# A hybrid encoder block: r's projections computed whole, eight pairs of half products instead of twelve, and the sums of x made during the first mixer

## The chip, the core and the metric

The kernel runs on one core of a Trainium2 chip, in float32 (matrix products in float32r). The metric is the device time of one execution in microseconds, the median of several runs. A profiled execution gives a trace beside it: what each engine did and when, and what ended each wait. The engines are TensorE (PE in the profile; its weight loads PEld), VectorE (DVE), ScalarE (ACT), GpSimd (POOL) and SyncE (SP, which here only issues DMA transfers).

## What is computed

One encoder block on x of 1024 tokens and 1024 features. Cut to what matters:

```python
h = rms_norm(x, norm_mix_g)
proj = h @ w_in        # gla q, k, v, r; low-rank gate codes; swa q, k, v; gate_a, gate_b
o = gla(q, k, v, gates, forward) + gla(q, k, v, gates, backward)    # chunked linear attention, 4 heads
y_gla = (rms_norm(o, out_g) * silu(r)) @ w_o_gla
y_swa = windowed_attention(rope(rms_norm(sq)), rope(rms_norm(sk)), sv, sinks) @ w_o_swa
merged = sigmoid(gate_a) * y_gla + sigmoid(gate_b) * y_swa
x = x + merged @ w_out
x = x + (silu(h2 @ w_gate) * (h2 @ w_up)) @ w_ffn_out               # h2 = rms_norm(x, norm_ffn_g)
```

The columns of `w_in` that this document speaks of are r, gate_a (ga) and gate_b (gb), 1024 columns each: eight rows of 128 columns, `r0` to `r7` and so on.

## The kernel before

Every float32 product is made of three: an operand is split into a high part in float32r and the rest, h and l, and `h*h + h*l + l*h` is accumulated (`mm3`, or three `matmul` lines). A split costs one copy on ScalarE (L69, L756, L787) and one subtraction on VectorE (L71, L757, L788). The unit of work is a product of 128 x 128 by 128 x 512 (128 partitions, 512 values each); x lies in SBUF as `xh[k][s]`, `xl[k][s]` for eight blocks k of features and two halves s of the tokens.

TensorE's order is written out by hand; the other engines' orders come from a scheduler at build time, and each engine then works its list strictly in order, SP's list of DMA issues too. The program runs through these stages:

1. The norm of x, the projections q0 and k0, the low-rank gate codes.
2. **The GLA mixer**, in 45 time slots (`slot`, L263). A slot runs the small stages of the linear attention that are due (gates, scores, outputs, backward outputs, transposes) and puts n products of *filling* between them. The filling (`dense`, L543) is a list of generators: the projections that are still to be made, in the order they are needed. `GF` gives n for three ranges of slots. Where a stage needs a projection that isn't there yet, `need` pulls more filling.
3. **The attention mixer** (SWA) in 22 slots, the same way, with `SF`. Keys are prepared in the first eight (`k_prep`, `k_turn`), a block of four query heads in each of sixteen (`a_prep`, `a_turn`, `a_scores`, `a_probs`, `a_out`). `inv_norm` (L589) gets the squares' sums of each head from ScalarE with `accum_out`.
4. **Half products.** r, ga and gb are not all made as filling. The twelve `PAIRS` of rows (m and m + 4 of r, ga, gb) are computed with seven products of half size instead of eight. Two of the seven (`first_halves`, L221: one row's weights by the first half of the tokens, over all eight blocks k; 24 products a pair) are filling. After the attention comes `xsums`: it loads x again, scales it, and forms sums and differences of its quarters, named T1, T2, 22, T3, T4. The filling that is left runs (`fill(1 << 30)`, L877), then `second_halves` makes the other five products of a pair, 12 each (60 a pair): Z with T1, X with T2, X with T3, Z with 22, X with T4. X and Z are accumulators in PSUM (tags `mm` and `ch`). VectorE reads X after T2 (u2, L845) before T3 accumulates on it, and the results (L835) go to memory. From the fifth pair on, `prep_a` follows each pair: it loads r and the linear attention's output for one block, applies the sigmoid (ScalarE) and splits the result.
5. The output projections of both branches, the merge, `w_out`, and the feed-forward block, with the same half products. The change doesn't touch them.

A weight tile `wr` has four buffers, its parts `wh` and `wl` five. In `proj_t` the eight weight units of a projection are used twice, for the two halves of the tokens. `wkeep` (L149) writes both parts to memory after the first split, from GpSimd's queue; `wagain` (L158) loads them for the second half.

Of the kernel before, what the change touches and what calls it, by code (L numbers as in the profile page):

```python
# [14 lines left out]
P = 128  # L15
T = 1024
KT = 8
# [8 lines left out]
GF = (27, 20, 12)  # L26
SF = (40, 17, 17)
# [5 lines left out]
def body(tc, i, out):  # L33
    nc = tc.nc
    with ExitStack() as root:
# [77 lines left out]
        scr = {}  # L113
        glas = ExitStack()
# [103 lines left out]
        PAIRS = [(nme, m, r0, r0 + 4) for nme, base in (("r", 8), ("ga", 16), ("gb", 24))  # L218
# [31 lines left out]
        def fill(n):  # L250

            while n > 0 and dense:
                try:
                    next(dense[0])
                    n -= 1
                except StopIteration:
                    dense.pop(0)

# [274 lines left out]
        def g_turn(hd, c):  # L533
# [6 lines left out]
            for j in range(2):  # L540
# [4 lines left out]
                  proj_t("sq1", 4), first_halves()]  # L545
# [12 lines left out]
        with tc.manual_schedule(engines={mybir.EngineType.PE}):  # L558
            fill(24)
            for t in range(last + 1):  # L560
                n = GF[0] if t < 24 else GF[1] if t < NH * NC + 3 else GF[2]
                slot([(lambda v=at[t, j]: v[0](*v[1:])) if (t, j) in at else None for j in (0, 5, 4, 3, 2, 1)], n)
# [26 lines left out]
        def inv_norm(raw, n, sq, scale, epsv, eps_t):  # L589
            ss = sw.tile([P, n], F32, tag=f"ss{n}", name=nm("ss"))  # L590
            for h in range(n):
                nc.scalar.activation(sq[:, h], raw[:, h], AF.Square, accum_out=ss[:, h:h + 1])
# [147 lines left out]
        with tc.manual_schedule(engines={mybir.EngineType.PE}):  # L740
            for t, v in enumerate(todo):
                v.sort(key=lambda e: order.index(e[0]))
                slot([lambda e=e: e[0](*e[1:]) for e in v], SF[0] if t < 2 else SF[1] if t < 2 * KT + 2 else SF[2])
# [47 lines left out]
        def xsums(k):  # L791
            b = {}
            for q, kq, s in ((11, k, 0), (12, k, 1), (21, k + 4, 0), (22, k + 4, 1)):
                tag = f"n{q}{k if s == 0 else k % 2}"
                b[q] = tp.tile([P, HT], F32, tag=tag, name=nm(tag))
                nc.sync.dma_start(out=b[q], in_=i["xT"][kq, s])
                nc.vector.scalar_tensor_tensor(b[q], b[q], g1[:, kq:kq + 1], rstd[:, s * HT:(s + 1) * HT],
                                               op0=ALU.mult, op1=ALU.mult)
            nc.vector.tensor_tensor(b[12], b[12], b[11], op=ALU.subtract)
            XT["T1"].append(xsplit(xp, f"xh{k}1", f"xl{k}1", b[12]))  # L800
            XT["22"].append(xsplit(xp, f"xh{k + 4}1", f"xl{k + 4}1", b[22]))
            nc.vector.tensor_tensor(b[22], b[22], b[12], op=ALU.subtract)
            XT["T2"].append(xsplit(tp, f"t2h{k}", f"t2l{k}", b[22]))
            nc.vector.tensor_tensor(b[11], b[22], b[11], op=ALU.subtract)
            nc.vector.tensor_tensor(b[21], b[21], b[22], op=ALU.subtract)
            raws.append((b[11], b[21]))

        def xsums_late(k):
            XT["T3"].append(xsplit(xp, f"xh{k}0", f"xl{k}0", raws[k][0]))
            XT["T4"].append(xsplit(xp, f"xh{k + 4}0", f"xl{k + 4}0", raws[k][1]))  # L810

        nturn = [0]

        def ntile():
            q, k = divmod(nturn[0] % 8, 4)
            nturn[0] += 1
            tag = f"n{(11, 21)[q]}{k}"
            return tp.tile([P, HT], F32, tag=tag, name=nm("nt"))

        def put(key, t):  # L820
            d = scratch("_".join(map(str, key)))
            nc.sync.dma_start(out=d, in_=t)
            scr[key] = d

        def second_halves(f):
# [3 lines left out]
            r11, r21 = rawload(i["w_f"][a, 0], True), rawload(i["w_f"][b, 0], True)  # L829
            r12, r22 = rawload(i["w_f"][a, 1], False), rawload(i["w_f"][b, 1], False)  # L830
            Z, X = chtile((P, HT)), mmtile()

            def result(key, bank, add):
                t = stage()
                nc.vector.tensor_tensor(t, bank, add, op=ALU.add)  # L835
                put(key, t)

            s1 = comb(r21, r22, ALU.add)
            product(Z, wsplit(s1, 512), XT["T1"], 4, True, False)
            p5 = ntile()  # L840
            nc.vector.tensor_tensor(p5, Z, p1, op=ALU.add)
            s2 = comb(s1, r11, ALU.subtract)
# [3 lines left out]
            s3 = comb(r11, r21, ALU.subtract)  # L846
            product(X, wsplit(s3, 512), XT["T3"], 4, False, False)
            result((f"{nme}{m + 4}", 1), X, p5)
            s4 = comb(r12, s2, ALU.subtract)
            product(Z, wsplit(s4, 512), XT["22"], 4, False, True)  # L850
            result((f"{nme}{m}", 1), Z, u2)
            product(X, wsplit(r22, 512), XT["T4"], 4, False, True)
# [21 lines left out]
        with tc.manual_schedule(engines={mybir.EngineType.PE}):  # L874
            for k in range(4):
                xsums(k)
            fill(1 << 30)  # L877
            for k in range(4):
                xsums_late(k)
# [450 lines left out]
```

## Time and profile before

| | us |
|---|---|
| median of 3 runs | 1740.34 (1736.09 to 1740.75) |
| the profiled execution | 1737.7 |
| its span, first to last instruction | 1735.9 |
| TensorE busy | 1664.8 (96%) |
| VectorE busy | 1252.4 (72%) |
| ScalarE busy | 876.2 (50%) |
| GpSimd busy | 43.6 (3%) |

The page divides the span into 40 slices of 43.4 us and gives the busy share of each in tenths. A row of the stretches ("windows") has the length, then for each engine its busy time and number of instructions, the granted TensorE clock as a share of full speed, the DMA engines' share and their GB/s. A row of the waits has the instruction that waited, what released it, the total, the count and the longest. A row of the timeline has start, duration, engine, line, operation, output and inputs, and in brackets the idle time ahead of it and its releaser. A releaser is inferred, and where the engine named was done long before, it was another. Matmuls are pipelined: a product lasts 0.39 us in the timeline, though the next starts 0.23 us after it.

### The profile page before, as it was taken

Reading aid. Unit: us, or ns where it says so; the run is one execution under the profiler, and the core shown is the slowest. Engines: PE = TensorE matmul, PEld = TensorE weight load, DVE = VectorE, ACT = ScalarE, POOL = GpSimd, SP = SyncE. Lnnn points to the kernel's source line nnn. Section 1 sums busy time; section 2 is a strip of 40 time slices with the busy share of each in tenths; the row PEclk is TensorE's granted clock in tenths of the full one; section 3 lists DMA queues with packets and bytes.
Section 4 is the critical chain, followed back from the end, with each engine's and each line's share of the span. In section 5 each row is a group of like instructions: output and inputs, shape, how many; then the busy total and the mean of one; then the engine's idle time right before and its main releaser. Section 6 shows DMA issues by size and latency. Waiting matters only on the chain.

```text
span 1735.9 us, 23918 instructions
## 1 busy us (share of the span) xinstructions
PE 1664.8 (96%) x7740; PEld 1371.7 (79%) x7740; DVE 1252.4 (72%) x2586; ACT 876.2 (50%) x1957; POOL 43.6 (3%) x84
## 2 busy tenths in 40 slices
PE   9999999997999949988999999999999999999999
PEld 7788888886778737767788888888888888888887
DVE  8658687746898596665666466988777788789755
ACT  7546777765898642222455455733333333354442
POOL 1001010110000000000000000000000000000000
PEclk9999999998999979999999999999999999999999
DMA  7646566678243455444676455435223445396433
GB/s 274 214 140 196 181 194 207 213 241 282 91 141 110 145 183 170 150 141 148 222 224 194 151 161 161 128 128 163 92 103 130 149 135 175 127 334 207 133 116 116
DMA packets 174973, 293.85 MB, mean 169 GB/s; under 512 B 20510, under 2 KB 45854, under 8 KB 174848
## 3 DMA queue, kind: packets, MB, share of 16 engines
q1 hardware_dynamic: 168448, 271.35, 48.6%
q0 software_dynamic: 6400, 20.98, 3.3%
q8 instruction: 61, 1.00, 0.3%
q14 instruction: 64, 0.52, 0.1%
HBM read 201.02 MB, written 91.23 MB: 168 GB/s over the span
## 4 chain that ended last, share of the span: by engine, by line
PE 79%; DVE 9%; ACT 6%; DMA 4%; issue 2%; SPq 1%; ACTq 0%; DVEq 0%
PE mm L75 27%; PE mm L777 7%; PE mm L779 7%; PE mm L778 7%; PE mm L1148 7%; PE ch L75 6%; PE ch L1148 5%; PE ch L777 3%; PE ch L779 3%; PE ch L778 3%; PE mm L238 2%; DMA st<-r 2%; ACT p L692 1%; DMA wr<-in_w_f_dram 1%; DMA kvr<-skv 1%
## 5 line engine op out<-in xcount | busy, mean ns | idle before, releaser
L756 ACT ACTIVATE wh<-ws 128x512 fp32r<-128x512 f32 x136 | 86.0, 633 | 216.0 <-PE mm L778 106.2
L69 ACT ACTIVATE wh<-wr 128x512 fp32r<-128x512 f32 x190 | 119.0, 630 | 109.3 <-PE mm L75 85.3
L71 DVE TENSOR_TENSOR wl<-wr,wh 128x512 fp32r<-128x512 f32 x190 | 130.2, 687 | 43.1 <-ACT wh L69 40.7
L75 PE MATMUL mm<-wl,xh 128*128 128x512 f32 x320 | 129.4, 404 | 0.0
L75 PE MATMUL mm<-wh,xh 128*128 128x512 f32 x320 | 128.6, 402 | 0.1
L75 PE MATMUL mm<-wh,xl 128*128 128x512 f32 x320 | 128.4, 401 | 0.0
L757 DVE TENSOR_TENSOR wl<-ws,wh 128x512 fp32r<-128x512 f32 x136 | 93.2, 686 | 13.5 <-ACT wh L756 13.4
L756 ACT ACTIVATE wh<-wr 128x512 fp32r<-128x512 f32 x64 | 40.6, 634 | 113.8 <-issue 49.7
L756 ACT ACTIVATE wh<-a 128x512 fp32r<-128x512 f32 x66 | 41.9, 634 | 91.0 <-PE ch L1148 42.3
L757 DVE TENSOR_TENSOR wl<-a,wh 128x512 fp32r<-128x512 f32 x66 | 45.5, 691 | 40.1 <-ACT wh L756 39.0
L75 PEld LDWEIGHTS mm<-wh,xl 128*128 128x128 f32 x320 | 61.2, 191 | 10.4
L1148 PE MATMUL mm<-hh,wh 128*128 128x512 f32 x176 | 68.6, 390 | 0.5 <-DVE c L1086 0.5
L75 PEld LDWEIGHTS mm<-wh,xh 128*128 128x128 f32 x320 | 61.1, 191 | 10.0 <-ACT st L213 0.5
L1148 PE MATMUL mm<-hh,wl 128*128 128x512 f32 x176 | 68.5, 389 | 0.0
L1148 PE MATMUL mm<-hl,wh 128*128 128x512 f32 x176 | 68.5, 389 | 0.0
L75 PEld LDWEIGHTS mm<-wl,xh 128*128 128x128 f32 x320 | 61.3, 192 | 8.7
L238 PE MATMUL mm<-xh,wh 128*128 128x512 f32 x96 | 40.3, 420 | 19.9 <-ACT xh L787 19.9
L777 PE MATMUL mm<-xh,wh 128*128 128x512 f32 x96 | 40.9, 426 | 18.5 <-DVE nt L845 18.5
L770 DVE TENSOR_TENSOR ws<-wr,wr 128x512 f32<-128x512 f32 x68 | 46.9, 690 | 14.3 <-DMA wr<-in_w_f_dram 6.4
L1121 DVE TENSOR_TENSOR hl<-hr,hh 128x512 fp32r<-128x512 f32 x77 | 52.8, 687 | 5.6 <-ACT hh L1120 5.5
L75 PE MATMUL mm<-oah,wh 128*128 128x512 f32 x128 | 50.5, 395 | 3.1 <-ACT oah L787 3.1
L1120 ACT ACTIVATE hh<-hr 128x512 fp32r<-128x512 f32 x77 | 47.7, 619 | 8.1 <-DMA hr<-B 4.2
(552 smaller groups left out, 5120.3 us busy)
## 6 DMA issues: line engine op xcount, KB each, us to landing
wr<-in_w_fi_dram SPq DMA_DIRECT2D x102, 256.0 KB, 2.9
wr<-in_w_f_dram SPq DMA_DIRECT2D x88, 256.0 KB, 3.5
B<-c SPq DMA_DIRECT2D x44, 256.0 KB, 2.1
T<-st SPq DMA_DIRECT2D x44, 256.0 KB, 2.6
a<-in_w_fo_dram SPq DMA_DIRECT2D x44, 256.0 KB, 5.2
hr<-T SPq DMA_DIRECT2D x44, 256.0 KB, 2.6
wr<-in_w_t_dram SPq DMA_DIRECT2D x40, 256.0 KB, 3.2
wh<-wh POOLq DMA_DIRECT2D x40, 256.0 KB, 3.3
```

Source lines behind the costliest of these rows:

```text
L69: nc.scalar.activation(h, raw, AF.Copy)
L71: nc.vector.tensor_tensor(l, raw, h.bitcast(F32), op=ALU.subtract)
L75: nc.tensor.matmul(o, a, b, start=start, stop=stop)
L238: nc.tensor.matmul(Y[q], w[:, c], x, start=f0, stop=f1, skip_group_check=True)
L756: nc.scalar.activation(h, src, AF.Copy)
L757: nc.vector.tensor_tensor(l, src, h.bitcast(F32), op=ALU.subtract)
L777: nc.tensor.matmul(o, h[:, c], x[kk][0], start=start and kk == 0, stop=False, skip_group_check=True)
L778: nc.tensor.matmul(o, h[:, c], x[kk][1], start=False, stop=False, skip_group_check=True)
L779: nc.tensor.matmul(o, l[:, c], x[kk][0], start=False, stop=kk == nk - 1, skip_group_check=True)
L1120: nc.scalar.activation(h, r, AF.Copy)
L1121: nc.vector.tensor_tensor(l, r, h.bitcast(F32), op=ALU.subtract)
L1148: nc.tensor.matmul(ys[m], a[:, c], b, start=f0, stop=f1, skip_group_check=True)
```

## The change

- r is no longer among the pairs. Its eight rows are made whole (`proj_f`, 48 products a row) as filling, after `sq1` and before `first_halves`. `PAIRS` has the eight pairs of ga and gb.
- The sums of x are formed during the GLA mixer's first eight slots (`x_sums`) and written to memory; after the attention `xpart` loads them and splits them, and the first twelve are mixed with the filling that is left, `fill(4)` after each.
- A pair's products come in the order T1, T2, 22, T3, T4, and the T1 product of the next pair is placed ahead of T4. `prep_a` follows each of the eight pairs.
- The filling's numbers: 40 a slot in the first eight slots of the GLA mixer, then 27, 21 and 12; 60 in the first two slots of the attention, then 28 and 15.
- In `inv_norm` ScalarE makes one square of all heads, and VectorE sums them with a reduction.
- `wkeep` stores through SP instead of GpSimd, and GpSimd's DMA scratch is made smaller, which leaves room for the new tiles.

```diff
-GF = (27, 20, 12)
-SF = (40, 17, 17)
+GF = ((8, 40), (24, 27), (35, 21), (1 << 30, 12))
+SF = ((2, 60), (18, 28), (1 << 30, 15))
...
-                nc.gpsimd.dma_start(out=d, in_=v.bitcast(F32))
+                nc.sync.dma_start(out=d, in_=v.bitcast(F32))
...
-        PAIRS = [(nme, m, r0, r0 + 4) for nme, base in (("r", 8), ("ga", 16), ("gb", 24))
+        PAIRS = [(nme, m, r0, r0 + 4) for nme, base in (("ga", 16), ("gb", 24))
...
-                  proj_t("sq1", 4), first_halves()]
+                  proj_t("sq1", 4)] + [proj_f(f"r{m}", 8 + m) for m in range(8)] + [first_halves()]
+
+        xn = glas.enter_context(tc.tile_pool(name="xn", bufs=4))
...
+        def x_norm(k, s):
+            t = xn.tile([P, HT], F32, tag="xn", name=nm("xn"))
+            nc.sync.dma_start(out=t, in_=i["xT"][k, s])
+            nc.vector.scalar_tensor_tensor(t, t, g1[:, k:k + 1], rstd[:, s * HT:(s + 1) * HT],
+                                           op0=ALU.mult, op1=ALU.mult)
+            return t
+
+        def x_diff(key, k, d, a, b):
+            nc.vector.tensor_tensor(d, a, b, op=ALU.subtract)
+            put((key, k), d)
+
+        def x_sums(j):
+            k, late = divmod(j, 2)
+            if not late:
+                a, b = part[k] = x_norm(k, 0), x_norm(k, 1)
+                x_diff("xT1", k, b, b, a)
+                return
+            a, b = part.pop(k)
+            c = x_norm(k + 4, 1)
+            put(("x22", k), c)
+            x_diff("xT2", k, b, c, b)
+            x_diff("xT3", k, a, b, a)
+            c = x_norm(k + 4, 0)
+            x_diff("xT4", k, c, c, b)
...
+                if t < 8:
+                    x_sums(t)
...
-            for h in range(n):
-                nc.scalar.activation(sq[:, h], raw[:, h], AF.Square, accum_out=ss[:, h:h + 1])
+            nc.scalar.activation(sq, raw, AF.Square)
+            nc.vector.tensor_reduce(ss, sq, axis=mybir.AxisListType.X, op=ALU.add)
...
+        def xpart(q, k):
+            r = tp.tile([P, HT], F32, tag="xr", name=nm("xr"), bufs=8)
+            nc.sync.dma_start(out=r, in_=scr[f"x{q}", k])
+            pool, th, tl, d = homes[q]
+            XT[q].append(xsplit(pool, th.format(k + d), tl.format(k + d), r))
...
+        def second_first(f):
...
+            g.s1 = comb(g.r21, g.r22, ALU.add)
+            g.Z = chtile((P, HT))
+            product(g.Z, wsplit(g.s1, 512), XT["T1"], 4, True, False)
+
+        def second_rest(f):
...
+            nc.vector.tensor_tensor(p5, g.Z, p1, op=ALU.add)
+            X = mmtile()
+            s2 = comb(g.s1, g.r11, ALU.subtract)
+            product(X, wsplit(s2, 512), XT["T2"], 4, True, False)
+            u2 = ntile()
+            nc.vector.tensor_tensor(u2, X, p1, op=ALU.add)
+            s4 = comb(r12, s2, ALU.subtract)
+            product(g.Z, wsplit(s4, 512), XT["22"], 4, False, True)
+            result((f"{nme}{m}", 1), g.Z, u2)
+            s3 = comb(g.r11, g.r21, ALU.subtract)
+            product(X, wsplit(s3, 512), XT["T3"], 4, False, False)
+            result((f"{nme}{m + 4}", 1), X, p5)
+            if f + 1 < len(PAIRS):
+                second_first(f + 1)
+            product(X, wsplit(g.r22, 512), XT["T4"], 4, False, True)
+            result((f"{nme}{m + 4}", 0), X, p1)
...
-            for k in range(4):
-                xsums(k)
+            for q in ("T1", "T2", "22"):
+                for k in range(4):
+                    xpart(q, k)
+                    fill(4)
             fill(1 << 30)
+            second_first(0)
...
             for f in range(len(PAIRS)):
-                second_halves(f)
-                if f >= 4:
-                    prep_a(0, f - 4)
+                second_rest(f)
+                prep_a(0, f)
...
+    nc = _bacc.Bacc("TRN2", target_bir_lowering=False, num_devices=1, dynamic_dma_scratch_size=1024)
```

VectorE's order where the attention has ended and the last filling runs, before: `n` are x's quarters (L797 scales, L799 to L805 form the sums), `xl` and `t2l` their splits, and L241 is the read of a bank that the filling then goes on accumulating in.

```order
L797 SCALAR_TENSOR_TENSOR n_2058_8362<-n_2058_8362,g_70,rstd 128x512
L804 TENSOR_TENSOR n_2047_8331<-n_2050_8340,n_2047_8331 128x512
L788 TENSOR_TENSOR t2l_2056_8354<-n_2050_8340,t2h_2055_8353 128x512
L805 TENSOR_TENSOR n_2049_8337<-n_2049_8337,n_2050_8340 128x512
L797 SCALAR_TENSOR_TENSOR n_2059_8365<-n_2059_8365,g_70,rstd 128x512
L797 SCALAR_TENSOR_TENSOR n_2060_8368<-n_2060_8368,g_70,rstd 128x512
L799 TENSOR_TENSOR n_2058_8362<-n_2058_8362,n_2057_8359 128x512
L241 TENSOR_TENSOR st_8417<-mm_8247,rstd 128x512
```

The same place in the changed kernel, where L826 splits what was loaded (`xr`) and L247 is the read of a bank:

```order
L826 TENSOR_TENSOR xl_2079_8687<-xr_8684,xh_2078_8686 128x512
L247 TENSOR_TENSOR st_8711<-mm_8612,rstd 128x512
L826 TENSOR_TENSOR xl_2082_8697<-xr_8694,xh_2081_8696 128x512
L826 TENSOR_TENSOR xl_2085_8707<-xr_8704,xh_2084_8706 128x512
L71 TENSOR_TENSOR wl_8801<-wr_8797,wh_8799 128x512
L826 TENSOR_TENSOR xl_2092_8727<-xr_8724,xh_2091_8726 128x512
L247 TENSOR_TENSOR st_8751<-mm_8613,rstd 128x512
L826 TENSOR_TENSOR t2l_2095_8737<-xr_8734,t2h_2094_8736 128x512
L826 TENSOR_TENSOR t2l_2098_8747<-xr_8744,t2h_2097_8746 128x512
L247 TENSOR_TENSOR st_8793<-mm_8755,rstd 128x512
```

Before, 36 rows stood between two reads of banks; now two to four do, and the sums are gone from here.

VectorE's order within a pair with `prep_a`, before: `nt` from `ch` is p5, L870 the multiplication of r by its sigmoid (`sg`), L845 is u2, L871 and L788 the rest of `prep_a`, `ws` and `wl` the combined weights and their low parts for products ahead.

```order
L841 TENSOR_TENSOR nt_9235<-ch_9215,nt_9205 128x512
L757 TENSOR_TENSOR wl_9348<-ws_9345,wh_9347 128x512
L870 TENSOR_TENSOR st_9195<-st_9195,sg_9197 128x512
L845 TENSOR_TENSOR nt_9255<-mm_9216,nt_9205 128x512
L871 SCALAR_TENSOR_TENSOR st_9193<-st_9193,og,st_9195 128x512
```

And in the changed kernel, where L864 is p5, L869 u2, L896 the multiplication by the sigmoid, and L843 a result (from Z, `ch`, after the product with 22; from X, `mm`, after T4 of the pair before in the first such row, after T3 in the last):

```order
L864 TENSOR_TENSOR nt_9202<-ch_9149,nt_9198 128x512
L795 TENSOR_TENSOR wl_9279<-ws_9275,wh_9278 128x512
L808 TENSOR_TENSOR ws_9403<-wr_9399,wr_2272_9401 128x512
L843 TENSOR_TENSOR st_9182<-mm_9076,nt_9070 128x512
L795 TENSOR_TENSOR wl_9295<-wr_2210_9145,wh_9294 128x512
L869 TENSOR_TENSOR nt_9223<-mm_9204,nt_9198 128x512
L795 TENSOR_TENSOR wl_9336<-ws_9333,wh_9335 128x512
L808 TENSOR_TENSOR ws_9461<-ws_9403,wr_9397 128x512
L896 TENSOR_TENSOR st_9188<-st_9188,sg_9190 128x512
L843 TENSOR_TENSOR st_9243<-ch_9149,nt_9223 128x512
```

u2 now stands ahead of the multiplication by the sigmoid. After these rows come L897, `wl`, `ws`, the split `oal`, and the result of T3.

SP's order at the start of the GLA mixer in the changed kernel: L67 loads a weight unit (`wr`), L160 stores the two parts of an earlier one (GpSimd's queue did this before), L561 loads x for the sums.

```order
L561 DMA xn_712<-in_xT_dram 128x512
L160 DMA wh_0_530<-wh_526 128x512
L561 DMA xn_723<-in_xT_dram 128x512
L160 DMA wl_0_532<-wl_528 128x512
L160 DMA wh_1_540<-wh_536 128x512
L160 DMA wl_1_542<-wl_538 128x512
L160 DMA wh_2_550<-wh_546 128x512
L160 DMA wl_2_552<-wl_548 128x512
L160 DMA wh_3_572<-wh_568 128x512
L160 DMA wl_3_574<-wl_570 128x512
L67 DMA wr_632<-in_w_t_dram 128x512
```

Before, SP's list had the loads of eight units in a row here. Now the fifth stands behind the stores of the first four.

More of the change, by code (lines that the diff above doesn't have):

```diff
@@ L257, in fill, with share @@
                     dense.pop(0)
+        def share(plan, t):
+            return next(n for end, n in plan if t < end)
         def need(key):
@@ L789, in xsplit @@
             return h, l
[L791 to L806, printed above, removed]
@@ L827, in second_halves @@
+        def second_rest(f):
+            nme, m, a, b = PAIRS[f]
+            g = pend.pop(f)
             p1 = ntile()
             nc.sync.dma_start(out=p1, in_=scr[f"{nme}{m}", "p1"])
[L829 to L836, printed above, removed]
```

50 lines of the change are left out of this document (22 added, 28 removed).

## The prediction

> **What bounds the kernel now.** I read the page's slices first, then the busy time of each engine by stretches, then TensorE's waits, then the timelines at the two largest gaps.
>
> ```profile
> span 1735.9 us, 23918 instructions
> ...
> PE   9999999997999949988999999999999999999999
> ```
>
> TensorE is the bound almost everywhere; its lower digits stand between 390 and 860 us. The stretches below are cut at events of the program: the GLA mixer with its filling, the attention mixer (and its middle by itself), the filling that is left, the twelve pairs, and a long piece of what follows.
>
> ```profile
> core 0: us, PE busy (x) PEld busy (x) DVE busy (x) ACT busy (x) POOL busy (x), PEclk, DMA share, GB/s
> 60.00:403.50 343.50, 339.69 (x1862) 288.78 (x1860) 226.53 (x634) 221.41 (x617) 34.66 (x64) 1.00 0.62 201
> 403.50:598.40 194.90, 178.48 (x904) 144.68 (x903) 158.97 (x564) 165.30 (x530) 0.00 (x0) 0.96 0.42 133
> 480.00:540.00 60.00, 59.42 (x325) 49.54 (x324) 56.99 (x193) 58.88 (x192) 0.00 (x0) 1.00 0.46 141
> 598.40:638.20 39.80, 19.86 (x78) 15.94 (x77) 35.88 (x57) 18.76 (x30) 0.00 (x0) 0.74 0.70 231
> 638.20:835.30 197.10, 175.56 (x725) 140.65 (x724) 125.96 (x196) 47.34 (x76) 0.00 (x0) 0.96 0.47 148
> 860.00:1520.00 660.00, 660.00 (x2909) 545.87 (x2909) 486.73 (x780) 279.64 (x464) 0.00 (x0) 1.00 0.46 149
> ```
>
> The last row gives the price of a 128x512 product with nothing in its way: 660 us / 2909 = **0.227 us**. With it the other rows become losses.
>
> - Attention: 194.90 - 178.48 = 16.4 us idle, and a mean clock of 0.96 costs about 0.04 x 194.9 = 7.8 more: **24 us**.
> - The filling that is left: 39.8 us for 78 products (17.7): **22 us**.
> - The twelve pairs: 197.1 us for 12 x 60 products (163.4): **34 us**.
> - Up to 403.5 only 343.5 - 339.7 = **4 us** are lost.
>
> ```profile
> PE mm L238 <- ACT xh L787: 19.9, 1, 19.9
> PE mm L777 <- DVE nt L845: 18.5, 11, 2.5
> PE ch L634 <- issue: 4.3, 1, 4.3
> ```
>
> These are the waits of the three losing stretches. The first of them reads differently in the timelines of TensorE and VectorE:
>
> ```profile
> 612.92 0.39 PE L238 MATMUL mm<-xh,wl 128*128 128x512 f32 x1
> 633.25 0.77 PE L238 MATMUL mm<-xh,wh 128*128 128x512 f32 x1 [19.94 <-ACT xh L787]
> 633.82 0.63 PE L238 MATMUL mm<-xl,wh 128*128 128x512 f32 x1
> 634.24 0.63 PE L238 MATMUL mm<-xh,wl 128*128 128x512 f32 x1
> 607.23 0.75 DVE L797 SCALAR_TENSOR_TENSOR n<-n,g,rstd 128x512 f32<-128x512 f32 x1
> ...
> 632.42 0.69 DVE L241 TENSOR_TENSOR st<-mm,rstd 128x512 f32<-128x512 f32 x1
> 633.02 1.29 DVE L788 TENSOR_TENSOR xl<-n,xh 128x512 fp32r<-128x512 f32 x2
> ```
>
> The profile names ScalarE, but the product at 633.25 goes on accumulating in a bank that VectorE has to read first (L241, ended at 633.11). That read is 0.7 us of work, queued behind the sums of x that began at 607.23. VectorE starts a 128x512 operation every 0.60 us (632.42 to 633.02). And after the gap products start 0.42 us apart instead of 0.227; with about ten of them, a gap of over 2 us costs some 2 us more in the clock.
>
> **The change part by part.**
>
> *Products.* A pair costs 84 products (24 + 60), two whole rows 96. Four pairs become whole: 4 x 12 = 48 more, 48 x 0.227 = **+10.9 us**. Nothing hides them, since TensorE is the bound.
>
> *The sums of x, early.* VectorE's 16 scalings (0.75, L797) and 16 sums (0.69, L653 below), 23 us, move to the first eight slots of the GLA mixer. VectorE is busy 226.5 of 343.5 us there, and the filling of these slots grows from 27 to 40 products. Beside them go 16 loads and 20 stores, and the 80 stores of kept weights move from POOL's queue to SP's.
>
> ```profile
> wr<-in_w_t_dram SPq DMA_DIRECT2D x40, 256.0 KB, 3.2
> wh<-wh POOLq DMA_DIRECT2D x40, 256.0 KB, 3.3
> 603.68 0.80 SPq L796 DMA_DIRECT2D n<-in_xT_dram  x2
> ```
>
> SP then has in one line: a load, two stores that wait for that load's split, the next load. Below, this costs nothing, since weights are loaded up to four buffers ahead; it cannot gain, because nothing waits for POOL's stores and only 4 us are lost there. Above, the 36 new transfers hold back the loads behind them by their whole time to issue, 36 x 0.40 (0.80 for two) = 14 us. I take **+4**, nearer to the low end, because SP is late for no product in that stretch today.
>
> [...] No row here shows the kept stores on SP.
>
> *Attention.* The first two slots get 60 products instead of 40, the sixteen after them 28 instead of 17. In the program's order 498 filling products stand between the first transpose of the keys and the last product of the attention, against 320; the 178 x 0.227 = 40 us are only moved here. They lie on waits like the 4.3 us above.
>
> ```profile
> L712 ACT ACTIVATE ph<-ch 128x512 fp32r<-128x512 f32 x44 | 23.9, 595 | 1.5 <-PE ch L709 1.5
> L592 ACT ACTIVATE sq<-qr 128x128 f32<-128x128 f32 x64 | 19.3, 314 | 5.2 <-DMA qr<-sq 2.8 <-DVE qn L610 2.3
> L592 ACT ACTIVATION_READ_ACCUMULATOR sq<-qr 128x1 f32 x64 | 13.2, 206 | 0.0
> L653 DVE TENSOR_TENSOR qn<-qn,sq 128x512 f32<-128x512 f32 x16 | 11.0, 690 | 0.0
> ```
>
> From 480 to 540 ScalarE is busy 58.9 of 60 us, VectorE 57.0, TensorE 59.4: all three are near their end. The norm of q takes 4 x (0.314 + 0.206) = 2.1 us of ScalarE per block now, and one square of about 0.6 us (L712) afterwards. VectorE gets a reduction instead, which this trace doesn't have. Below, it costs nothing where VectorE waits anyway; above, twice a 128x512 operation, 1.4 us. I take 0.69, the row of L653, which passes as many values. A block then has ScalarE 1.5 us lighter, VectorE 0.7 heavier and TensorE 11 x 0.227 = 2.5 heavier. So TensorE becomes the longest in the later slots, and VectorE stays close to it in the eight that also prepare keys. Of the 24 us lost I leave 8 (ends 3 and 20): **-16**.
>
> [...]
>
> *The filling that is left.* 99 products follow the last product of the attention (which ended at 598.3), 22.5 us of cover. The loads of the sums still wait for the attention's memory, so I take today's delays: issue 5.3 us after that product (603.68), data 8.9 after it (607.23). In VectorE's new order no bank read stands behind more than two or three splits, so the 22 us go: **-22**.
>
> *The first pair.* From the first split of x to the weights of the third product (with s4) VectorE's order has 36 rows; at 0.60 they take 22 us and end 8.9 + 0.5 + 22 = 31 us after the attention. TensorE is there after 22.5 + 24 x 0.227 = 28 us. It waits 3 us, and the clock adds 2: 5 are left.
>
> *The other pairs.* Rows of TensorE, SP, ScalarE and VectorE around one gap:
>
> ```profile
> 740.37 0.39 PE L779 MATMUL mm<-t2h,wl 128*128 128x512 f32 x1
> 742.91 0.47 PE L777 MATMUL mm<-xh,wh 128*128 128x512 f32 x1 [2.15 <-DVE nt L845]
> 736.46 0.42 SPq L867 DMA_DIRECT2D st<-r  x1
> 740.81 0.63 ACT L869 ACTIVATE sg<-st 128x512 f32<-128x512 f32 x1 [2.27 <-DMA st<-r]
> 735.36 0.69 DVE L835 TENSOR_TENSOR st<-mm,nt 128x512 f32<-128x512 f32 x1 [0.70 <-PE mm L779]
> ...
> 741.47 0.69 DVE L870 TENSOR_TENSOR st<-st,sg 128x512 f32<-128x512 f32 x1 [2.10 <-ACT sg L869]
> 742.08 0.68 DVE L845 TENSOR_TENSOR nt<-mm,nt 128x512 f32<-128x512 f32 x1
> ```
>
> The third product (T3) needs u2 (L845), the read of the second one's bank. It stands behind the sigmoid of r, whose load is issued at 736.46. Afterwards the product with x22 lies between, 12 x 0.227 = 2.7 us, and u2 stands ahead of r's multiplication in VectorE's order. What is late next: T3's result must be read before T4 begins. The sigmoid ends 6.1 us after the last pair's T4 (735.3 to 741.4). From there seven rows of 0.60 put the end of T3's read at 10.3 us, and T4 begins at 48 x 0.227 = 10.9. It holds by half a microsecond, so I leave 0.5 us for each of seven pairs. With the first pair, 5 + 3.5 = 8.5 of 34 us are left (ends 4 and 27): **-25**. The wait for the last `prep_a` after the pairs stays.
>
> **Sum**, against the profiled execution's own 1737.7 us (the span of 1735.9 and 1.8 around it; the median of the runs, 1740.3, is 2.6 above): 1737.7 + 10.9 + 4 - 16 - 22 - 25 = 1689.6, so **1690 us**.
>
> **The rivals.**
>
> 1. *VectorE becomes the bound in the pairs.* For it: 17 rows of 0.60 are 10.2 of a pair's 13.6 us, in one order, with half a microsecond of slack at T4. Against: nothing but the load of r has to be late. If seven pairs keep today's 2.2 us and the clock's 2 instead of 0.5, that is 26 us more: **1716**.
> 2. *The gap only moves.* The sums come back from memory through the same queue. If the twelve loads that the first three products need land one after another, 12 x 3.2 = 38 us, the third product's operands come at 5.3 + 38 + 1.2 = 45 instead of 31 us, and the clock adds 2: **1706**. Against: eight buffers for them, and loads overlap at 603.68.
> 3. *Slower: SP starves the GLA mixer's filling.* A kept unit feeds 12 products, and TensorE now takes one in about 4.0 us (343.5 us for some 1040 filling products). If the next load goes out only when the stores before it have landed, a unit takes 3.2 + 3.3 = 6.5 us, and 40 units cost 40 x 2.5 = 100 us: **1790**. It outweighs the gains from 5.2 us a unit on. Against: four buffers, and a DMA share of 0.62.
> 4. *Everything closes*, all terms at their good ends (0, -21, -22, -30): **1676**.
>
> **How the numbers follow.** My forecast has 0.60, rival 1 0.20, rival 2 0.07, rival 3 0.05, rival 4 0.08. The range of 1672 to 1718 takes in all but rival 3 and a stack of several bad ends; the unknown prices (the reduction's 11 us, SP's 10) lie within it. A measurement of this kernel tells 0.3% (5.2 us) from no change. Faster by over that: 0.93, which is every case but rival 3 and a stack of bad ends on rival 1. Within it: 0.02. Slower: 0.05.
>
> **What would show it.** In the changed profile the wait of 19.9 us is gone, and no gap over 4 us stands between the attention's last product and the first pair's third; T3 no longer waits for u2; the keys' first transposes come at about 428 us, the attention's last product at about 646, the pairs' end at about 788 instead of 835. I am wrong if weight loads hold TensorE before 428 us (rival 3), if the pairs' products wait over 1 us each for VectorE (rival 1), or if the stages behind the pairs are not as long as before.

## The result, and the profile after

| | before | after |
|---|---|---|
| median of 4 runs, us | 1740.34 (1736.09 to 1740.75) | 1682.82 (1679.58 to 1685.03) |
| the profiled execution, us | 1737.7 | 1679.58 |
| its span, us | 1735.9 | 1677.3 |
| granted clock, mean | 0.983 | 0.996 |

The ratio of the times is 0.967 (95% interval 0.965 to 0.970). The forecast was 1690, with a range of 1672 to 1718.

The slices of the page, after, as they were shown of before:

```profile
span 1677.3 us, 23798 instructions
...
PE 1655.2 (99%) x7788; PEld 1372.9 (82%) x7788; DVE 1237.9 (74%) x2570; ACT 857.1 (51%) x1809; POOL 0.2 (0%) x4
...
PE   9999999999999998999999999999999999999999
```

One digit is still below 9, the sixteenth, where the pairs begin. The stretches, cut at the same events of the program (the columns are those of the table of before):

```profile
60.00:425.80 365.80, 362.55 (x1968) 308.26 (x1967) 253.06 (x694) 228.34 (x626) 0.00 (x0) 1.00 0.69 228
425.80:634.10 208.30, 206.60 (x1079) 173.75 (x1078) 167.76 (x564) 153.21 (x390) 0.00 (x0) 1.00 0.36 114
634.10:656.60 22.50, 22.50 (x100) 18.40 (x98) 14.49 (x23) 10.23 (x17) 0.00 (x0) 1.00 0.88 289
656.60:776.00 119.40, 114.37 (x486) 93.04 (x486) 93.38 (x147) 43.66 (x72) 0.00 (x0) 0.97 0.65 215
```

The attention now has 1.7 us of idle time and a full clock, and the filling that is left has none. Only the pairs still lose: 119.4 us for 480 products (109.0). TensorE's longest waits of the whole kernel:

```profile
PE ch L815 <- ACT wh L794: 4.6, 2, 2.6
PE mm L75 <- ACT oah L825: 3.2, 1, 3.2
PE ch L75 <- DVE lrS L313: 1.9, 1, 1.9
PE mm L75 <- DMA wl<-wl: 1.2, 1, 1.2
```

The waits of 19.9 us (last filling) and 18.5 us (T3 for u2) are gone. Where the time came from, stretch by stretch, at 0.227 us for each product that was added or taken away:

| stretch | length, us | products | its products' time | what else | predicted |
|---|---|---|---|---|---|
| to the first key transposes | 403.5 to 425.8 | +89 | +20.2 | **+2.1** | +4 |
| attention | 194.9 to 208.3 | +175 | +39.7 | **-26.3** | -16 |
| filling that is left | 39.8 to 22.5 | +22 | +5.0 | **-22.3** | -22 |
| pairs | 197.1 to 119.4 | -240 | -54.5 | **-23.2** | -25 |
| behind the pairs | 900.6 to 901.3 | 0 | 0 | **+0.7** | 0 |

The products are +10.4 in sum (the prediction had 10.9; these rows hold 46 of the 48 more that the page counts, 7788 against 7740), and all together makes -58.6, the difference of the spans. Before's first key transposes begin at 408.0, after a wait of 4.3 us; its stretch is cut where that wait begins, at 403.5, so the wait counts with the attention.

### The profile page after: what moved, and what is told of

Read it like the earlier page. It is cut to its first block, busy times and chain, and to the rows that moved or that the text cites. A ratio compares the mean times of both kernels' runs of the same rounds, so it can differ in the third digit from the quotient of the medians.

```text
span 1677.3 us, 23798 instructions
## 1 busy us (share of the span) xinstructions
PE 1655.2 (99%) x7788; PEld 1372.9 (82%) x7788; DVE 1237.9 (74%) x2570; ACT 857.1 (51%) x1809; POOL 0.2 (0%) x4
## 4 chain that ended last, share of the span: by engine, by line
PE 91%; DVE 3%; DMA 3%; ACT 2%; issue 1%; SPq 0%; ACTq 0%; DVEq 0%
PE mm L75 35%; PE ch L75 8%; PE mm L815 7%; PE mm L816 7%; PE mm L817 7%; PE mm L1177 7%; PE ch L1177 5%; PE ch L815 3%; PE ch L817 3%; PE ch L816 3%; PE mm L244 2%; PE ch L747 1%; DMA xr<-xT 1%; PE ch L546 0%; PE ch L697 0%
## 5 line engine op out<-in xcount | busy, mean ns | idle before, releaser
L71 DVE TENSOR_TENSOR wl<-wr,wh 128x512 fp32r<-128x512 f32 x198 | 135.7, 686 | 32.0 <-ACT wh L69 29.1
L794 ACT ACTIVATE wh<-ws 128x512 fp32r<-128x512 f32 x120 | 75.5, 631 | 148.7 <-PE mm L816 84.6
L75 PE MATMUL mm<-xh,wh 128*128 128x512 f32 x256 | 102.5, 401 | 0.3 <-ACT wh L69 0.3
L75 PE MATMUL mm<-xl,wh 128*128 128x512 f32 x256 | 102.0, 398 | 0.3 <-DVE xl L323 0.3
L795 DVE TENSOR_TENSOR wl<-ws,wh 128x512 fp32r<-128x512 f32 x120 | 82.1, 685 | 12.8 <-ACT wh L794 12.8
L75 PE MATMUL mm<-xh,wl 128*128 128x512 f32 x256 | 88.6, 399 | 0.0
L75 PEld LDWEIGHTS mm<-wl,xh 128*128 128x128 f32 x320 | 60.5, 189 | 12.6 <-DMA wl<-wl 1.6
L75 PEld LDWEIGHTS mm<-xl,wh 128*128 128x128 f32 x256 | 48.2, 188 | 7.6 <-DVE xl L323 0.6
L75 PEld LDWEIGHTS mm<-xh,wh 128*128 128x128 f32 x256 | 48.2, 188 | 7.4 <-ACT wh L69 0.5
```

The source lines that it names most:

```text
L71: nc.vector.tensor_tensor(l, raw, h.bitcast(F32), op=ALU.subtract)
L75: nc.tensor.matmul(o, a, b, start=start, stop=stop)
L794: nc.scalar.activation(h, src, AF.Copy)
L795: nc.vector.tensor_tensor(l, src, h.bitcast(F32), op=ALU.subtract)
```

## The experiments

Kernels measured together share a chip and its runs of before, whose median was 1739.6 us for e1 to e4, 1739.6 for e5 to e8, 1738.3 for e9 to e11 and 1740.6 for e12; the ratios are to these. The profiled execution is one of the runs, and not always near their median: e1's took 1740.7 us and was the slowest of its six. Four events of each profiled execution, in us: the first key transposes (A), the copy of the attention's last output (B), the last filling product (C), the last product of the pairs (D):

| kernel | median, us | ratio to before, 95% interval | A | B | C | D |
|---|---|---|---|---|---|---|
| before | 1740.3 | | 408.0 | 598.4 | 638.0 | 835.1 |
| after | 1682.8 | 0.9652 to 0.9695 | 425.8 | 634.3 | 656.4 | 775.7 |
| e1 SP stores only | 1733.8 | 0.9931 to 0.9978 | 404.1 | 593.2 | 632.8 | 836.3 |
| e2 new norm only | 1738.1 | 0.9978 to 1.0014 | 409.4 | 598.2 | 637.2 | 834.4 |
| e3 old norm | 1685.2 | 0.9654 to 0.9707 | 428.1 | 638.8 | 660.8 | 781.1 |
| e4 old attention filling | 1696.0 | 0.9728 to 0.9760 | 420.8 | 611.3 | 681.4 | 791.3 |
| e5 old order in a pair | 1702.5 | 0.9762 to 0.9809 | 425.3 | 633.8 | 655.8 | 798.4 |
| e6 late sums | 1708.3 | 0.9797 to 0.9839 | 419.9 | 629.0 | 652.3 | 802.3 |
| e7 twelve pairs | 1694.3 | 0.9712 to 0.9763 | 412.5 | 598.5 | 615.8 | 792.3 |
| e8 first pair eased | 1671.3 | 0.9586 to 0.9629 | 423.8 | 633.2 | 655.4 | 770.8 |
| e9 ten pairs | 1686.8 | 0.9676 to 0.9723 | 422.0 | 623.6 | 637.5 | 786.5 |
| e10 spread sums | 1675.3 | 0.9605 to 0.9656 | 431.1 | 641.1 | 663.1 | 777.6 |
| e11 e8 again | 1673.4 | 0.9593 to 0.9646 | 426.6 | 636.4 | 658.4 | 774.6 |
| e12 sums at the end | 1674.4 | 0.9607 to 0.9660 | 429.9 | 638.4 | 661.3 | 776.7 |

### What closed the attention: the norm or the filling (e2, e3, e4)

e2 makes this edit in the kernel before, e3 takes it back in the changed one:

```diff
-            for h in range(n):
-                nc.scalar.activation(sq[:, h], raw[:, h], AF.Square, accum_out=ss[:, h:h + 1])
+            nc.scalar.activation(sq, raw, AF.Square)
+            nc.vector.tensor_reduce(ss, sq, axis=mybir.AxisListType.X, op=ALU.add)
```

> The kernel before, with only the new norm of the heads: one square on ScalarE and one reduction on VectorE. Theory A, the attention's loss was closed by more filling between its stages: 1740 within 3 us, since VectorE gets 0.7 us a block and nothing covers it better. Theory B, ScalarE's four squares and four accumulator reads were what the attention waited for: most of its 24 us go, so 1718 to 1728, and the stretch of the attention falls from 195 to about 175 us.

> The changed kernel with the old norm of the heads put back (ScalarE squares with sums). Theory A (filling covers): ScalarE has 1.5 us more a block beside 4.5 us that TensorE is busy with filling, so 1683 to 1688. Theory B (the norm was the bound): the attention loses 12 to 24 us again, so 1695 to 1707.

e4 takes the attention's numbers back in the changed kernel:

```diff
-SF = ((2, 60), (18, 28), (1 << 30, 15))
+SF = ((2, 40), (1 << 30, 17))
```

> The changed kernel with the attention's old filling numbers (40 in two slots, then 17); the some 200 products not placed there run after the attention. Theory A (filling covers the stages' waits): the attention loses 12 to 26 us again, mostly as gaps of TensorE and a lower granted clock, so 1695 to 1709. Theory B (the norm did it): 1683 within 5 us.

The norm alone does nothing measurable (1738.1 against 1739.6, the interval holds 1), and its removal costs 2.4 us with intervals that overlap. The filling does it. e4 rose to 1696.0, as its theory A had it. Its attention and the filling left after it, from the stretches, and its waits in the attention:

```profile
420.80:611.50 190.70, 175.46 (x903) 141.77 (x902) 157.09 (x556) 149.58 (x384) 0.00 (x0) 0.98 0.33 102
611.50:681.60 70.10, 70.10 (x311) 58.00 (x310) 41.24 (x65) 27.46 (x45) 0.00 (x0) 1.00 0.80 263
681.60:791.50 109.90, 109.90 (x485) 90.76 (x484) 83.67 (x130) 34.73 (x56) 0.00 (x0) 1.00 0.56 187
...
PE ch L697 <- DVE mx L715: 4.8, 3, 2.8
PE ch L75 <- DVE mx L715: 3.3, 7, 1.8
PE ch L75 <- DVE kTl L675: 2.4, 1, 2.4
```

With 176 products less (40.0 us) the attention is only 17.6 us shorter (208.3 to 190.7): 22.4 us of its waits and of the lower clock after them (0.98) are back, 13.5 of them as idle time (15.2 us against 1.7). The third row is a gain that nobody had asked for: with 70 us of filling ahead of them the pairs lose nothing (109.9 us, no idle time). So the time rose by 13 us, not by 22.

Most of this happens while the keys are prepared. The stretch from the first key transposes to the last, in before, in after and in e4:

```profile
403.50:482.00 78.50, 65.90 (x312) 53.50 (x311) 66.75 (x270) 64.22 (x236) 0.00 (x0) 0.89 0.45 149
425.80:500.00 74.20, 74.20 (x389) 63.14 (x388) 73.29 (x271) 57.80 (x155) 0.00 (x0) 1.00 0.42 136
420.80:495.40 74.60, 63.25 (x311) 50.08 (x310) 70.48 (x273) 57.57 (x153) 0.00 (x0) 0.95 0.42 134
```

TensorE was idle for 12.6 us of it in before (4.3 of them the wait ahead of the first transposes) and for 11.4 in e4. In after it never was, although VectorE was busy 73.3 of the 74.2 us.

The reduction's price is in the groups of VectorE of the changed kernel (count, busy us, mean ns):

```profile
L630 DVE TENSOR_REDUCE ss<-sq 128x4 f32<-128x512 f32 x16 | 10.9, 681 | 0.0
```

The reduction takes 0.68 us, against the 0.69 that the prediction took and the 1.4 of its upper end. A `tensor_tensor` of the same 512 values takes 0.69 us (L71, 686 ns on the page).

### SP's queue and the sums in the GLA mixer (e1, e10, e12)

e1 is the kernel before with one edit:

```diff
-                nc.gpsimd.dma_start(out=d, in_=v.bitcast(F32))
+                nc.sync.dma_start(out=d, in_=v.bitcast(F32))
```

> The kernel before, with the stores of the kept weights issued from SP instead of GpSimd and nothing else changed. Theory A, the prediction's +4: SP's one line holds the loads back, the stretch up to the first key transposes grows by 2 to 5 us, so 1742 to 1746. Theory B, only the time to issue counts: SP has room, 1740 within 2 us. Rival C, each load waits for the landing of the stores ahead of it: 1790 or more.

All three miss: by the medians the kernel is faster, by 3.8 to 12.0 us. The products reach the first key transposes at the same time (404.1 against 403.5), but the 4.3 us that before then waited are gone. The operands of these transposes go back to the constants of the attention. SP's rows for the last of them and for the first keys and values, in before and then in e1:

```profile
388.76 2.01 SPq L67 DMA_DIRECT2D wr<-in_w_f_dram  x2
...
396.82 0.94 SPq L62 DMA_DIRECT2D sink<-in_sink_dram  x1
397.81 0.97 SPq L625 DMA_DIRECT2D kvr<-skv  x1
```

```profile
392.42 0.43 SPq L62 DMA_DIRECT2D sink<-in_sink_dram  x1
392.89 0.43 SPq L625 DMA_DIRECT2D kvr<-skv  x1
```

In e1 they go out 4 to 5 us earlier, with no weight loads just ahead of them and at half the time to issue, and the attention ends 5.2 us earlier (593.2 against 598.4). Where the median's gain lies stays open, since this execution was not faster as a whole: its pairs took 203.5 us from C to D against before's 197.1, which used the 5.2 us up.

e10 and e12 were to find the price of the sums in the first slots, on top of e8 (below):

```diff
-                if t < 8:
-                    x_sums(t)
+                if t < 24 and t % 3 == 1:    # e10
+                    x_sums(t // 3)
+                if 34 <= t < 42:             # e12
+                    x_sums(t - 34)
```

> The kernel of e8 with the sums of x formed in every third GLA slot from the second on (8 of the first 24) instead of in the first eight. Theory A (the sums cost the GLA mixer 4 to 6 us, as the first key transposes of e6 at 419.9 against 425.8 say, because VectorE's small stages of the first slots stand behind them): 1666 to 1669 and the first transposes at 420 to 422. Theory B (those 4 us are only the spread of single profiles): within 2 us of e8.

> The kernel of e8 with the sums of x formed in GLA slots 34 to 41 instead of 0 to 7. From 340 us on VectorE is busy less than half of the time in e8 (8.95 of 20 us from 340 to 360), against 45.7 of 60 from 60 to 120 us. Theory A (the sums cost 26 products' time in the first 120 us, since the small stages wait behind them and behind 1.9 times the DMA traffic): most of 5.9 us comes back, 1666 to 1669, with the first key transposes at 419 to 422. Theory B (their loads and stores, at a DMA share of 0.6 to 0.9 there, hold back the weights and the constants of the attention): 1673 or more.

Neither tells its theories apart, since the sums hardly moved; that e12's median lies in theory B's range says nothing for B. The subtractions of the sums in e8 and in e12 (count, least, median and longest ns, first and last start in us):

```profile
L567 DVE TENSOR_TENSOR xn<-xn,xn x16: 669/689/693, 45.6 to 109.4; 128x512 f32<-128x512 f32 x16
```

```profile
L567 DVE TENSOR_TENSOR xn<-xn,xn x16: 666/684/695, 46.9 to 129.0; 128x512 f32<-128x512 f32 x16
```

Only TensorE's order is that of the code. The scheduler orders VectorE's and SP's work, and it began the sums at the same place wherever the call stands; x and `rstd` are there from the start. The last of them ran some 20 us later, and the first key transposes came at 431.1 and 429.9, later than in any execution with the sums in the first slots (428.1 at most); why is not shown. The price of the sums comes from e6, which has none in the GLA mixer, and the same 2203 products up to the key transposes. The stretch from 60 to 120 us, in after and then in e6:

```profile
60.00:120.00 60.00, 58.89 (x297) 49.50 (x296) 44.14 (x97) 26.60 (x59) 0.00 (x0) 1.00 0.88 296
```

```profile
60.00:120.00 60.00, 60.00 (x309) 50.88 (x309) 33.74 (x84) 30.81 (x71) 0.00 (x0) 1.00 0.49 157
```

After has VectorE 10 us busier, 1.9 times the DMA traffic, and 12 products less, with 14 less in the 60 us ahead of it: 26 products are 5.9 us. e6 reaches the transposes at 419.9 instead of 425.8, and five executions with that part of the program alike lie between 423.8 and 428.1. So the sums cost about 6 us there (4 to 8, from one execution of e6). Whether VectorE or the DMA traffic makes the cost is not shown. A place for them that costs less wasn't found.

### The order of a pair (e5)

```diff
             u2 = ntile()
             nc.vector.tensor_tensor(u2, X, p1, op=ALU.add)
+            s3 = comb(g.r11, g.r21, ALU.subtract)
+            product(X, wsplit(s3, 512), XT["T3"], 4, False, False)
+            result((f"{nme}{m + 4}", 1), X, p5)
             s4 = comb(r12, s2, ALU.subtract)
             product(g.Z, wsplit(s4, 512), XT["22"], 4, False, True)
             result((f"{nme}{m}", 1), g.Z, u2)
-            s3 = comb(g.r11, g.r21, ALU.subtract)
-            product(X, wsplit(s3, 512), XT["T3"], 4, False, False)
-            result((f"{nme}{m + 4}", 1), X, p5)
-            if f + 1 < len(PAIRS):
-                second_first(f + 1)
             product(X, wsplit(g.r22, 512), XT["T4"], 4, False, True)
             result((f"{nme}{m + 4}", 0), X, p1)
+            if f + 1 < len(PAIRS):
+                second_first(f + 1)
```

> The changed kernel with the old order of a pair's products: T1, T2, T3, 22, T4, and T1 of the next pair after T4. Theory A (the order closed the pairs' gaps: u2 stands behind the sigmoid of r again, with no product in between): each of eight pairs waits 0.9 to 2.4 us ahead of T3 and pays up to 2 us in the clock, 1.1 to 4.2 a pair by the pair lengths of the kernel before, so the pairs take 126 to 150 us instead of 117 and the time is 1692 to 1716, nearer to the upper end. Theory B (r came out of the pairs, its results lie in memory long before, and that closed the gaps): only the bare read of the bank is left, 1683 to 1692.

Theory A, in the middle of its range. The edit takes both moves back, the place of the product with 22 and that of the next pair's T1; they were not tried one by one. The wait of before is back at its place, and the pairs take 140.1 us from the first product to the last instead of 117.0:

```profile
PE mm L815 <- DVE nt L869: 15.7, 8, 3.3
```

### The sums late (e6)

```diff
-                if t < 8:
-                    x_sums(t)
...
+            for t in range(8):
+                x_sums(t)
             for q in ("T1", "T2", "22"):
                 for k in range(4):
                     xpart(q, k)
                     fill(4)
```

> The changed kernel with the sums of x formed after the attention instead of in the first eight slots of the GLA mixer; they are still written to memory and loaded again. Theory A (VectorE's 32 operations of the sums at this place cost the 22 us): 19 us of VectorE and a way through memory of 5 to 6 us come back ahead of the splits, TensorE's cover is the same, and the filling or the first pair waits some 20 us: 1697 to 1710. Theory B (the filling between the loads, four products after each, keeps VectorE's reads of banks near, and that alone closes the gap): the filling doesn't wait, the first pair waits under 8 us more: 1683 to 1691.

Theory A. The filling hardly waits (1.1 us, theory B's part of it holds), but T1's operands come late, block by block:

```profile
PE ch L812 <- ACT xh L822: 30.3, 3, 11.2
```

The pairs take 149.7 us instead of 117.0, the GLA mixer gives 6 back, and 25.5 us are lost.

### r as half products again (e7, e9)

e7 puts r back among the pairs, with the old filling numbers of both mixers (`GF` 27, 20, 12 and `SF` 40, 17) and with `prep_a` from the fifth pair on; e9, on top of e8, does it for two of r's four pairs:

```diff
-        PAIRS = [(nme, m, r0, r0 + 4) for nme, base in (("ga", 16), ("gb", 24))
+        PAIRS = [(nme, m, r0, r0 + 4) for nme, base in (("r", 8), ("ga", 16), ("gb", 24))
```

> The changed kernel with r as four pairs again (twelve pairs, 48 products or 10.9 us less) and the old filling numbers of both mixers, since 288 filling products are gone. New order of a pair, early sums, new norm and SP stores stay. Theory A (the whole rows of r pay for themselves by covering the attention): the attention loses 12 to 24 us again, so 1684 to 1698, no faster than the changed kernel. Theory B (the other edits carry the gain, r as whole rows only costs): 1672 within 4 us.

> The kernel of e8 with two rows' pairs of r as half products again (ten pairs): 24 products less, 144 less filling, taken from the first eight GLA slots (33 for 40) and from the attention's slots 2 to 17 (24 for 28). Theory A (a filling product placed in the attention is worth 0.11 us on the average, 22.9 us for 202 in e4): 5.4 us gained, some 7 lost in the attention and some 2 elsewhere, 1671 to 1679. Theory B (the last products placed there cover nothing any more): 1664 to 1668.

e7 is 11.5 us slower with 10.9 us less to multiply. Its attention and its pairs:

```profile
412.50:598.60 186.10, 172.95 (x903) 140.72 (x902) 163.04 (x569) 152.75 (x394) 0.00 (x0) 0.99 0.44 145
...
616.00:792.50 176.50, 167.11 (x725) 137.69 (x724) 130.85 (x202) 59.03 (x94) 0.00 (x0) 0.97 0.59 196
```

Against after, the attention has 176 products (40.0 us) less and is 22.2 us shorter: 17.8 us are lost there. The first key transposes, at 412.5, come 9.0 us after before's 403.5 with one product more; with 27 filling products a slot instead of 40 the sums may cost more than the 6 us above. e9 misses both ranges on the side of A: 13.5 us over e11, the same base on the same chip. Its attention, its last filling and its pairs, and then e8's attention:

```profile
422.00:623.70 201.70, 195.70 (x1017) 162.20 (x1016) 165.32 (x551) 152.33 (x389) 0.00 (x0) 0.99 0.40 127
623.70:637.70 14.00, 14.00 (x64) 11.55 (x63) 11.34 (x18) 5.72 (x10) 0.00 (x0) 1.00 0.86 281
637.70:786.70 149.00, 141.15 (x605) 115.14 (x604) 113.11 (x176) 54.85 (x87) 0.00 (x0) 0.98 0.64 210
```

```profile
423.80:633.30 209.50, 207.40 (x1081) 173.79 (x1080) 168.87 (x568) 154.45 (x394) 0.00 (x0) 1.00 0.36 115
```

The attention lost 6.7 us by the same sum (64 products less are 14.5 us, and it is 7.8 shorter), as expected. But only 14.0 us of filling are left behind it, and the ten pairs take 149.0 us for 600 products (136.2): 12.8 lost against 6.4 in e8. And the first key transposes come 1.8 us earlier than e8's, 4.6 earlier than e11's, with 43 products (9.8 us) less, so 5 to 8 us are lost in the GLA mixer, where seven products a slot were taken from the slots that make the sums.

### The first pair (e8, e11)

What the changed kernel still waits for stands in these rows of TensorE and VectorE (start, duration, idle time in brackets):

```profile
658.72 0.50 PE L815 MATMUL ch<-xh,wh 128*128 128x512 f32 x1 [1.98 <-ACT wh L794]
669.40 0.50 PE L815 MATMUL ch<-xh,wh 128*128 128x512 f32 x1 [2.58 <-ACT wh L794]
656.66 0.68 DVE L826 TENSOR_TENSOR xl<-xr,xh 128x512 fp32r<-128x512 f32 x1
657.26 0.69 DVE L808 TENSOR_TENSOR ws<-wr,wr 128x512 f32<-128x512 f32 x1
664.54 2.29 DVE L826 TENSOR_TENSOR xl<-xr,xh 128x512 fp32r<-128x512 f32 x3 [0.16 <-ACT xh L825]
667.94 0.68 DVE L808 TENSOR_TENSOR ws<-wr,ws 128x512 f32<-128x512 f32 x1
```

Both sums of weights (`ws`) stand behind splits (`xl`) for products that come later: the first behind those for 22, the second (s4) behind those for T4. e8 moves them (`first_w` is the part of `second_first` ahead of its product), and makes the last two blocks of `prep_a` one pair earlier, the first three one pair later:

```diff
+                if q == "22":
+                    first_w(0)
...
-            for q in ("T3", "T4"):
-                for k in range(4):
-                    xpart(q, k)
...
             s4 = comb(r12, s2, ALU.subtract)
-            product(g.Z, wsplit(s4, 512), XT["22"], 4, False, True)
+            w4 = wsplit(s4, 512)
+            if f == 0:
+                for k in range(4):
+                    xpart("T3", k)
+            product(g.Z, w4, XT["22"], 4, False, True)
...
             result((f"{nme}{m + 4}", 1), X, p5)
+            if f == 0:
+                for k in range(4):
+                    xpart("T4", k)
...
-                prep_a(0, f)
+                for k in ((), (0,), (1,), (2, 3), (4,), (5, 6), (7,), ())[f]:
+                    prep_a(0, k)
```

> The changed kernel with three moves on VectorE and ScalarE: the weights of the first pair's T1 are combined ahead of the splits for the product 22, the splits for T3 come after the weights of the product 22 and those for T4 after T3, and the last block of prep_a is made one pair earlier. Theory A (the first pair's two waits, 2.0 and 2.6 us, are VectorE working in order through splits that nothing needs yet; with the cold clock behind each they cost 8 us, and the wait of 3.2 us after the pairs costs 4 to 5): 1670 to 1675. Theory B (T3's operands come too late from memory, the gap moves to T3): 1680 to 1685.

> The kernel of e8 once more, beside e10 on the same chip: 1671 within 3 us.

Theory A: 1671.3 and 1673.4, 0.6% below the changed kernel, with intervals that don't meet. This is the fastest version found.

```profile
655.60:771.00 115.40, 111.17 (x485) 90.41 (x484) 92.13 (x147) 43.51 (x72) 0.00 (x0) 1.00 0.68 229
771.00:800.00 29.00, 29.00 (x129) 24.02 (x128) 19.67 (x31) 15.06 (x27) 0.00 (x0) 1.00 0.78 257
```

Behind the pairs 896.2 us are left instead of 901.3. The pairs still lose 6.4 us, so the gap got smaller rather than closed. The three moves were not tried one by one.

## Why the prediction was right, and where it was off

**The shape.** TensorE was the bound, and most of what its idle time and clock said was lost came back. Three of the four terms beside the products came within 2 us; the attention was 10.3 us better than its term, which is about what the sum of 1689.6 was off the profiled execution's 1679.6. Some of the nearness is luck, since two terms were right in sum and not in their parts.

**Products, +10.9.** They are there (+10.4 by the counts of the rows), and they buy more than they cost: e7 without them is slower (1694.3 us against 1682.8).

**The sums early and SP, +4.** The sum was near (+2.1), its parts were not. The sums cost some 6 us, while the term gave 0 to 14 to the issue of transfers. The larger filling of the slots, whose gain the term left out, may give back the 4 us that before lost there (e6, one execution, stands 3.8 us ahead of before's 403.5 plus its 89 products). The stores on SP cost next to nothing there (e1: 404.1 us against 403.5).

**Attention, -16.** This is the step that failed in size: "Of the 24 us lost I leave 8". All of it went, and the gain of 26.3 lies beyond the term's good end of 21. That VectorE would stay near its end where keys are prepared was right: it was busy 73.3 of 74.2 us there. What failed is the step from there to a wait. TensorE was never idle in these 74.2 us, while in e4, with less filling and VectorE less busy (70.5 of 74.6 us), it was idle for 11.4. So the products between the stages decide whether TensorE waits, and the 8 us that were left for VectorE's sake didn't come. e4 gives the filling 22.4 of the 26.3 us. The rest is about the 4.3 of the wait ahead of the first transposes, which the prediction listed as one that filling would cover, and which e1 removes without filling. The range also held 11 us for the reduction, 16 of them at up to 1.4 us instead of 0.69; no run shows these 11 us, and the 16 took 0.68 us each in the mean.

**The filling that is left, -22.** Right in place and size (-22.3). In e6 the sums are back behind the attention, and the filling still waits only 1.1 us: the new order, four products after each load, is enough to keep it going. The sums' return costs 25.5 us all the same, in the first pair. So both moves are needed; the early sums with the old order of the filling were not tried.

**The first pair, 5 left, and 3.5 in the seven others.** The sum was near (8.5 against the 10.4 of the stretch), its division wasn't: nearly all of it lies in the first pair. The wait for s4 was foreseen as 3 us and measured 2.58. The 1.98 us ahead of T1 weren't: the prediction has no wait there. Behind each of these two waits eight products started 0.43 us apart, about 1.6 us more each time, where the prediction had 2. The seven other pairs have no wait. The half microsecond of slack that was counted on is there, in the rows of one pair:

```profile
728.43 0.63 ACT L895 ACTIVATE sg<-st 128x512 f32<-128x512 f32 x1 [1.91 <-DMA st<-r]
729.10 0.69 DVE L896 TENSOR_TENSOR st<-st,sg 128x512 f32<-128x512 f32 x1 [1.02 <-ACT sg L895]
732.90 0.68 DVE L843 TENSOR_TENSOR st<-mm,nt 128x512 f32<-128x512 f32 x1
734.02 0.39 PE L815 MATMUL mm<-xh,wh 128*128 128x512 f32 x1
```

VectorE still waits for the sigmoid, and reads T3's result until 733.58; T4 begins at 734.02, 0.44 us later, with no wait. Rival 1, the same mechanism with the slack gone, didn't come, but it was 0.44 us away in this pair. In e8's profile it shows in two of the eight pairs: T4 waited 0.44 and 0.95 us for the read of T3's result.

**The other rivals.** The gap did move to the first pair, but with 4.6 us and not the 17 of rival 2: SP issued the twelve loads within 12 us (638.96 to 651.03), where the rival had them take 38 one after another. Rival 3 fell with e1. Rival 4 (1676) is nearest to the profiled execution, since the attention went beyond its good end.

## What to carry to other kernels

Where the bounding engine waits between short stages, count how much independent work stands between them before looking at the stages' own cost: here 176 products were worth 22 us of waits, and making r whole, 48 products more, put where waits were, made the kernel faster. A busy share near 1 on a second engine doesn't say that the bound waits for it: with VectorE busy 73.3 of 74.2 us TensorE lost nothing, and with VectorE busy 70.5 of 74.6 us and less filling it lost 11.4. And look up in the trace where moved work really ran, before reading the time: in two experiments here the call was moved and the work hardly was.

## What was unexpected of the hardware

A gap of TensorE of about 1.9 us is followed by slow products in one execution and not in the next. The same instructions, in the changed kernel and then in e8:

```profile
50.22 0.63 PE L75 MATMUL mm<-wh,xl 128*128 128x512 f32 x1
50.65 0.63 PE L75 MATMUL mm<-wh,xh 128*128 128x512 f32 x1
```

```profile
49.77 0.40 PE L75 MATMUL mm<-wh,xl 128*128 128x512 f32 x1
50.01 0.39 PE L75 MATMUL mm<-wh,xh 128*128 128x512 f32 x1
```

Both come after a wait of 1.9 us for `lrS`; the first pair starts 0.43 us apart, the second 0.24. In e5 a gap of 1.79 us ahead of T3 had no slow products behind it, one of 1.85 had eight, and those of 3.0 and 3.3 us had all of the 12 slow. In the kernel before, four gaps of 2.06 to 2.29 us ahead of T3 had six to eight products 0.41 to 0.43 us apart behind them, and those of 2.39 and 2.46 had none. The prediction's limit of 2 us lies inside this zone, and its 2 us more for a gap over the limit, worked out from the one gap of 19.9 us, don't come behind every such gap. Eight products 0.43 us apart instead of 0.23 are 1.6 us. That this is one part of what separates executions of one kernel is the author's estimate; why a gap of this length is followed by slow products at one time and not at another is not shown.
